# A decoder layer on one core: v by the seven-product scheme, with sums of products formed in their PSUM banks

## The chip, the core and the metric

One core of one Trainium2 chip runs the whole program. The metric is the device time of one execution in microseconds (us). TensorE (PE) multiplies, VectorE (DVE), ScalarE (ACT) and GpSimd (POOL) do the elementwise work, SyncE (SP) issues most of the DMAs.

## The reference, cut to what matters

One layer on 1024 tokens of 1024 channels, all in fp32:

```python
u = rms_norm(x, norm_g)                      # (1024, 1024)
proj = u @ w_in                              # ten blocks of 1024 columns
xc, bg, cg, zc, q, k, v, za, g_conv, g_attn = split(proj)
y_conv = (silu(zc) * bg * causal_conv(cg * xc, conv_w)) @ w_out_conv
o = mixture_of_dilations(q, k, v)            # 16 heads of 64
y_attn = (silu(za) * o) @ w_out_attn
merged = sigmoid(g_conv + b1) * y_conv + sigmoid(g_attn + b2) * y_attn
return rms_norm(x + merged @ w_o, final_g)
```

The change is in the input projection `u @ w_in`: in the part that gives v, and in the nine other blocks of columns (the sections).

## The kernel before, in words

**Exact fp32 from pairs.** TensorE works on float32r operands. Every fp32 operand a is therefore split (`split`, L78 to L80) into a high part, cast by ScalarE, and a low part, the difference, by VectorE or GpSimd. A product of two operands is three matmuls: low times high, high times low, high times high.

**The stage of v** (about the first 130 us). Each of eight token tiles of 128 rows of x is normalised: ScalarE sums the squares, VectorE takes the reciprocal root in three small steps with a Newton step (`rstd_of`, L101 to L111) and scales the tile in two halves (L173); TensorE turns each half with four transposes (L176), and `split` stores the result in one of four quadrants of u transposed: b11 (channels 0 to 511, tokens 0 to 511), b12 (the same channels, tokens 512 to 1023), b21 and b22 (channels 512 to 1023). v = u w_v is then computed in four blocks of 256 columns, in each eight token tiles, for each eight steps of the contraction with three matmuls of 256 columns (L212 to L214): 4 x 8 x 8 x 3 = 768. ScalarE casts the result from PSUM, VectorE takes the low part, and a DMA stores both (L215 to L219). The weights of a block are loaded and split by `load_v`; the low parts of all of them but the first half of block 0 are GpSimd's. Behind the first four tiles of the last block `sums` (L182 to L200) forms, for a slice of 128 tokens, t1 = b12 - b11, t2 = b22 - t1, t3 = t1 - b11 and so on from the pairs; nine operations of VectorE, four casts of ScalarE, four low parts of GpSimd for each slice. t1 to t4 are operands of the sections.

**The sections.** `sec` computes two blocks of 128 output columns for all tokens by Strassen's scheme in Winograd's form: seven products of half the contraction and half the tokens in place of eight (84 matmuls of 512 columns, L250 to L252, for a pair; 36 pairs). Three products go to SBUF through ScalarE (`keep`, L255 to L258), four are added by VectorE to a stored one (`added`, L260 to L264), and three more additions combine the sums in SBUF (L271 to L273). Every product has a PSUM bank of its own (`bank()` hands out eight in turn).

**What follows** is the attention, 16 heads, then the merge of the two branches and the output projection; the change does not touch their code.

**What sets the order.** The Tile framework orders the instructions with its own simulation of the program (`schedule_with_timeline_sim=True`) and then gives each engine one list, which that engine works through strictly in order. So the place of an instruction in the list of its engine decides what it can hold up. DMAs of SP and POOL are issued in the order of those lists as well.

## Time and profile before

| | |
|---|---|
| median of 3 runs | 1351.56 us (1350.42 to 1355.43) |
| the profiled execution, span | 1349.6 us |
| TensorE busy | 1303.3 us, 97 % of the span, 6660 matmuls and transposes |
| VectorE, ScalarE, GpSimd busy | 915.8, 631.4, 265.3 us |
| mean granted TensorE clock | 0.987 of full speed |
| stage of v, from the first load to the first section | 0 to about 130 us |
| sections | about 130 to 820 us |

The profile is one execution; its span runs from the first to the last instruction and is 2.0 us below the median of the runs. Busy time is time in which an engine executes, so TensorE's 97 % leave 46.3 us in which it did not. The granted clock says how much of full speed the throttle allowed: 1.0 is 2.4 GHz, 0.5 is 1.2 GHz. In the lists below "L212" is line 212 of the kernel, `out<-in` are the program's names for the operands, and "[4.79 <-DVE v L80]" says that the engine waited 4.79 us and that the VectorE instruction of line 80 that wrote v ended the wait.

### The profile page before, as it was taken

Reading aid. Unit: us, or ns where it says so; the run is one execution under the profiler, and the core shown is the slowest. Engines: PE = TensorE matmul, PEld = TensorE weight load, DVE = VectorE, ACT = ScalarE, POOL = GpSimd, SP = SyncE. Lnnn points to the kernel's source line nnn. Section 1 sums busy time; section 2 is a strip of 40 time slices with the busy share of each in tenths; the row PEclk is TensorE's granted clock in tenths of the full one; section 3 lists DMA queues with packets and bytes.
Section 4 is the critical chain, followed back from the end, with each engine's and each line's share of the span. In section 5 each row is a group of like instructions: output and inputs, shape, how many; then the busy total and the mean of one; then the engine's idle time right before and its main releaser. Section 6 shows DMA issues by size and latency. Waiting matters only on the chain.

```text
span 1349.6 us, 18655 instructions
## 1 busy us (share of the span) xinstructions
PE 1303.3 (97%) x6660; PEld 1102.2 (82%) x6660; DVE 915.8 (68%) x1722; ACT 631.4 (47%) x1259; POOL 265.3 (20%) x191
## 2 busy tenths in 40 slices
PE   7988999999999999999999998799999999999997
PEld 7988888888888888887888886688888888788886
DVE  6486777777878788887766566576766776564325
ACT  5333444443534444343444466666777767332211
POOL 1153000000100101011000001534345446164000
PEclk8989999999999999999999999899999999999999
DMA  7214454441322223246332317976466565555302
GB/s 273 102 63 141 141 187 154 162 148 52 104 68 78 94 70 103 63 124 196 108 109 96 125 70 197 319 196 173 142 166 173 140 160 200 210 187 187 141 32 93
DMA packets 85892, 187.19 MB, mean 139 GB/s; under 512 B 8552, under 2 KB 33388, under 8 KB 85672
## 3 DMA queue, kind: packets, MB, share of 16 engines
q1 hardware_dynamic: 83000, 177.08, 42.4%
q0 software_dynamic: 2800, 8.94, 2.0%
q8 instruction: 52, 0.85, 0.3%
q14 instruction: 40, 0.33, 0.1%
HBM read 127.67 MB, written 58.31 MB: 138 GB/s over the span
## 4 chain that ended last, share of the span: by engine, by line
PE 85%; DMA 7%; DVE 4%; ACT 2%; issue 1%; POOL 0%; SPq 0%; DVEq 0%; ACTq 0%; POOLq 0%
PE bank L252 16%; PE bank L251 16%; PE bank L250 16%; PE bank L97 4%; PE bank L99 4%; PE bank L98 4%; PE bank L480 3%; PE bank L491 2%; PE bank L492 2%; PE bank L651 2%; PE bank L649 2%; PE bank L650 2%; PE bank L362 2%; PE bank L363 2%; PE bank L214 2%; PE bank L212 2%
## 5 line engine op out<-in xcount | busy, mean ns | idle before, releaser
L252 PE MATMUL bank<-t_hi,a_lo 128*128 128x512 f32 x576 | 223.6, 390 | 2.1 <-DVE a_lo L80 2.1
L250 PE MATMUL bank<-t_hi,a_hi 128*128 128x512 f32 x576 | 224.1, 389 | 0.0
L251 PE MATMUL bank<-t_lo,a_hi 128*128 128x512 f32 x576 | 224.1, 389 | 0.0
L250 PE MATMUL bank<-b_hi,a_hi 128*128 128x512 f32 x432 | 168.1, 389 | 0.0
L251 PE MATMUL bank<-b_lo,a_hi 128*128 128x512 f32 x432 | 168.1, 389 | 0.0
L252 PE MATMUL bank<-b_hi,a_lo 128*128 128x512 f32 x432 | 167.9, 389 | 0.0
L79 ACT CAST a_hi<-s 128x512 fp32r<-128x512 f32 x144 | 89.4, 621 | 138.9 <-PE bank L251 128.7
L80 DVE TENSOR_TENSOR a_lo<-s,a_hi 128x512 fp32r<-128x512 f32 x144 | 101.1, 703 | 68.9 <-ACT a_hi L79 68.3
L79 ACT CAST a_hi<-raw 128x512 fp32r<-128x512 f32 x108 | 67.0, 621 | 161.5 <-PE bank L251 146.5
L252 PEld LDWEIGHTS bank<-t_hi,a_lo 128*128 128x128 f32 x576 | 108.1, 188 | 25.3 <-DVE a_lo L80 2.9
L251 PEld LDWEIGHTS bank<-t_lo,a_hi 128*128 128x128 f32 x576 | 108.1, 188 | 22.5
L250 PEld LDWEIGHTS bank<-t_hi,a_hi 128*128 128x128 f32 x576 | 108.1, 188 | 22.4
L372 ACT ACTIVATE pr<-pr,nm 128x640 f32<-128x640 f32 (+7 forms) x128 | 100.1, 783 | 26.2 <-DVE nm L367 25.8
L263 DVE TENSOR_TENSOR sec_o<-bank,x 128x512 f32<-128x512 f32 x108 | 74.5, 690 | 43.2 <-PE bank L252 40.5
L367 DVE CUSTOM_DVE_ANT_0 pr<-bank,bias 128x512 f32<-128x512 f32 (+3 forms) x128 | 72.2, 570 | 41.8 <-PE bank L363 40.0
L252 PEld LDWEIGHTS bank<-b_hi,a_lo 128*128 128x128 f32 x432 | 81.1, 188 | 16.9
L251 PEld LDWEIGHTS bank<-b_lo,a_hi 128*128 128x128 f32 x432 | 81.1, 188 | 16.8
L250 PEld LDWEIGHTS bank<-b_hi,a_hi 128*128 128x128 f32 x432 | 81.1, 188 | 16.8
L480 PE MATMUL bank<-ident,pr 128*128 128x128 f32 x576 | 89.3, 277 | 1.2 <-ACT pr L372 1.0
L212 PE MATMUL bank<-v_hi,b_hi 128*128 128x256 f32 x256 | 75.0, 296 | 11.8 <-DVE v L80 9.7
L80 DVE TENSOR_TENSOR a_lo<-raw,a_hi 128x512 fp32r<-128x512 f32 x108 | 75.3, 697 | 14.5 <-ACT a_hi L79 14.5
L80 DVE TENSOR_TENSOR pp<-bank,pp 128x512 fp32r<-128x512 f32 x96 | 65.3, 689 | 19.8 <-ACT pp L79 19.1
(212 smaller groups left out, 2913.3 us busy)
## 6 DMA issues: line engine op xcount, KB each, us to landing
raw<-in_w_blk SPq DMA_DIRECT2D x72, 512.0 KB, 3.8
v_dram<-v SPq DMA_DIRECT2D x32, 256.0 KB, 2.2
qk_dram<-qk_hi SPq DMA_DIRECT2D x32, 256.0 KB, 3.1
qk_dram<-qk_lo SPq DMA_DIRECT2D x32, 256.0 KB, 2.9
q<-qk_dram SPq DMA_DIRECT2D x32, 256.0 KB, 6.2
kh<-qk_dram SPq DMA_DIRECT2D x32, 256.0 KB, 8.5
kl<-qk_dram SPq DMA_DIRECT2D x32, 256.0 KB, 7.4
g_dram<-sg SPq DMA_DIRECT2D x32, 256.0 KB, 2.0
```

Of the source, the lines that this page charges most:

```text
L79: nc.scalar.copy(hi, src)
L80: (eng or nc.vector).tensor_sub(lo, src, f(hi))
L97: nc.tensor.matmul(pt, whi[:, k, :], mhi[:, t], start=(k == 0), stop=False)
L98: nc.tensor.matmul(pt, whi[:, k, :], mlo[:, t], start=False, stop=False)
L212: nc.tensor.matmul(pv, mhi[:, kk, tt], hi[:, kk, :], start=(k == 0), stop=False)
L250: nc.tensor.matmul(pt, hi[:, k], mhi[:, k], start=k == 0, stop=False)
L251: nc.tensor.matmul(pt, hi[:, k], mlo[:, k], start=False, stop=False)
L252: nc.tensor.matmul(pt, lo[:, k], mhi[:, k], start=False, stop=k == H - 1)
L263: nc.vector.tensor_add(o, pt, v)
L367: nc.vector.tensor_tensor_reduce(pr[:, c0:c0 + m], sc[:, :m], bias[hd][:, off:off + m], 1.0, 3.0e38 if nm is None else nm, OP.add, OP.min, ...
L372: nc.scalar.activation(pr[:, :nk], pr[:, :nk], AF.Exp, bias=nm, scale=-1.0, accum_out=den[p][:, a, b:b + 1])
L480: nc.tensor.transpose(pt[:, j, i * P:(i + 1) * P], rows[b][:, (kb + j) * P:(kb + j + 1) * P], ident)
```

## The change

It does four things.

1. **v by the seven-product scheme.** The products now have 512 columns: a product is half of the contraction (four steps) for four token tiles and 512 columns of v, 4 x 4 x 3 = 48 matmuls, and seven products make 336. The first two (b11 and b21 with the weights' first column half) are done tile by tile, in turn with the normalisation of tiles 0 to 3; then tiles 4 to 7 are normalised, within `sums`, and the other five products follow, each for all four tiles. Weights are loaded in pieces of two contraction steps by 512 columns, and VectorE forms their sums.
2. **Sums of products in their banks.** A product may go on adding to a bank that has been read already: `start` is set on the first product alone. In v and in every pair of columns of the sections the scheme then needs three banks (`chain`, `side`, `own`): chain holds x1, then x1 + x6 (t2's product is added), then t3's, then t4's. Four additions of VectorE go in each pair, and ScalarE copies one more value (u2).
3. **u's sums from fp32 copies.** For tiles 4 to 7 ScalarE copies the transposed tile out of PSUM (c12, c22), and `sums` forms t1, t2 and t3 from these. b12 has no pair any more. Six operations of VectorE for a slice remain, besides the normalisation.
4. **Memory.** Two pools are gone, x tiles have three buffers instead of four, and `dynamic_dma_scratch_size=4096` is set.

The diff, cut to its core (the sums' arithmetic and the helpers stand in full, unchanged lines mostly left out):

```diff
...
-        def load_v(c):
-            wv[c] = []
-            raw = [wr.tile([P, H, 256], F32, name="raw") for _ in range(2)]
...
+        def piece(c, d, kh):
+            raw = wr.tile([P, 2, 512], F32, tag="raw", name="raw")
+            k = 4 * d + 2 * kh
+            nc.sync.dma_start(raw, w_v[c, :, k:k + 2, :])
+            return raw
+        def operand(raw, eng=None):
+            hi = p0.tile([P, 2, 512], F32R, name="v_hi", bufs=4)
+            lo = p0.tile([P, 2, 512], F32R, name="v_lo", bufs=4)
+            split(hi, lo, raw, eng)
+            return hi, lo
...
+        raws = [piece(0, 0, 0), piece(0, 0, 1)]
         load_x(1)
+        raws += [piece(0, 1, 0), piece(0, 1, 1)]
+        load_x(2)
+        a1 = [operand(r, nc.gpsimd if i else nc.vector) for i, r in enumerate(raws)]
...
         def sums(j):
+            c12 = p0.tile([P, H, P], F32, name="c12", bufs=1)
+            c22 = p0.tile([P, H, P], F32, name="c22", bufs=1)
+            for n, pt in enumerate(normed(H + j)):
+                nc.scalar.copy(c22 if n else c12, pt)
+                if n:
+                    into("b22", j, pt)
+            t1, t2, t4 = (p0.tile([P, H, P], F32, name="ts", bufs=3) for _ in range(3))
+            b11, b21 = of("b11", j), of("b21", j)
+            nc.vector.tensor_sub(t1, c12, b11[0])
+            nc.vector.tensor_sub(t1, t1, b11[1])
+            into("t1", j, t1, nc.gpsimd)
+            nc.vector.tensor_sub(t2, c22, t1)
+            into("t2", j, t2, nc.gpsimd)
+            nc.vector.tensor_sub(c12, c22, c12)
+            into("t3", j, c12, nc.gpsimd)
+            nc.vector.tensor_sub(t4, b21[0], t2)
+            nc.vector.tensor_add(t4, t4, b21[1])
+            into("t4", j, t4, nc.gpsimd)
...
+                nc.tensor.matmul(pt, bhi[:, k, tt], hi[:, i, :], start=first and k == 0, stop=False, **more)
...
+        for j in range(H):
+            for n, pt in zip(("b11", "b21"), normed(j)):
+                into(n, j, pt)
+            for kh in range(2):
+                prod(chain[j], "b11", j, kh, a1[kh], first=True)
+            x1.append(p0.tile([P, 512], F32, name="keep1", bufs=4))
+            nc.scalar.copy(x1[j], chain[j])
+            pt = bank(4, 2)
+            for kh in range(2):
+                prod(pt, "b21", j, kh, a1[2 + kh], first=True)
+            added(0, j, pt, x1[j])
+        sum_ = []
+        for kh in range(2):
+            r1, r2 = piece(1, 0, kh), piece(1, 1, kh)
+            nc.vector.tensor_add(r1, r1, r2)
+            sum_.append(r1)
+        for j in range(H):
+            sums(j)
...
+        product("t1", side, [operand(r) for r in sum_], first=True)
...
+        product("t2", chain, [operand(r) for r in sum_])
...
+        product("b22", side, [operand(r) for r in sum_])
+        for j in range(H):
+            added(0, H + j, side[j], u2[j])
...
+        product("t3", chain, ops)
+        for j in range(H):
+            added(1, H + j, chain[j], x5[j])
+        product("t4", chain, [operand(piece(1, 1, kh)) for kh in range(2)])
+        for j in range(H):
+            emit(1, j, chain[j])
...
-        x1 = keep("x1", a11, "b11")
-        yield 0, T1, added(a12, "b21", x1)
-        x5 = keep("x5", sm["s1"], "t1")
-        x7 = keep("x7", sm["s3"], "t3")
-        u2 = added(sm["s2"], "t2", x1)
-        nc.vector.tensor_add(x7, x7, u2)
-        nc.vector.tensor_add(u2, u2, x5)
-        nc.vector.tensor_add(x5, x7, x5)
-        yield 1, T2, x5
-        yield 1, T1, added(a22, "t4", x7)
-        yield 0, T2, added(sm["s4"], "b22", u2)
+        chain = bank()
+        prod(chain, a11, "b11", first=True)
+        x1 = keep("x1", chain)
+        own = bank()
+        prod(own, a12, "b21", first=True)
+        yield 0, T1, added(own, x1)
+        side = bank()
+        prod(side, sm["s1"], "t1", first=True)
+        x5 = keep("x5", side)
+        prod(chain, sm["s2"], "t2")
+        u2 = keep("u2", chain)
+        prod(side, sm["s4"], "b22")
+        yield 0, T2, added(side, u2)
+        prod(chain, sm["s3"], "t3")
+        yield 1, T2, added(chain, x5)
+        prod(chain, a22, "t4")
+        yield 1, T1, chain
...
-        "w_v": blocks(w_in[:, 6 * D:7 * D], 256),
+        "w_v": blocks(w_in[:, 6 * D:7 * D], 512),
...
-    nc = _bacc.Bacc("TRN2", target_bir_lowering=False, num_devices=1)
+    nc = _bacc.Bacc("TRN2", target_bir_lowering=False, num_devices=1, dynamic_dma_scratch_size=4096)
...
```

Line numbers in the lists of the changed kernel are those of its own code: L103 to L110 are `rstd_of`, L171 scales a tile, L79 takes a low part, L226 is `added` of v (vc is the sum, keep_212 the stored x1), L245, L262, L269 and L276 form sums of weights, L194 to L202 stand in `sums`, L314 to L316 are a section's three matmuls.

**First place: VectorE between the token tiles.** Before, from its list at tile 2, with the low part of v (v_425, straight from PSUM) of column block 0 in between:

```order
L111 TENSOR_SCALAR rs<-rs_t,rs_y 128x1
L104 TENSOR_SCALAR rs_a<-ss 128x1
L80 TENSOR_TENSOR v_425<-bank,v_425 128x4x64
L173 SCALAR_TENSOR_TENSOR xt<-xt,rs,gb 128x512 x2
L80 TENSOR_TENSOR b_lo<-bank,b_hi 128x4x128
L108 RECIPROCAL rs_y<-rs_r 128x1
L80 TENSOR_TENSOR b_lo<-bank,b_hi 128x4x128 x2
L110 SCALAR_TENSOR_TENSOR rs_t<-rs_y,rs_a 128x1
L80 TENSOR_TENSOR b_lo<-bank,b_hi 128x4x128
L111 TENSOR_SCALAR rs<-rs_t,rs_y 128x1
```

With the change, the list between tiles 0 and 1 and on to the addition of tile 1:

```order
L226 TENSOR_TENSOR vc<-bank,keep_212 128x512
L245 TENSOR_TENSOR raw<-raw 128x1024
L103 TENSOR_SCALAR rs_a<-ss 128x1
L79 TENSOR_TENSOR v_229<-vc,v_229 128x8x64
L107 RECIPROCAL rs_y<-rs_r 128x1
L109 SCALAR_TENSOR_TENSOR rs_t<-rs_y,rs_a 128x1
L110 TENSOR_SCALAR rs<-rs_t,rs_y 128x1
L245 TENSOR_TENSOR raw<-raw 128x1024
L171 SCALAR_TENSOR_TENSOR xt<-xt,rs,gb 128x512 x2
L79 TENSOR_TENSOR b_lo<-bank,b_hi 128x4x128 x2
L226 TENSOR_TENSOR vc<-bank,keep_276 128x512
```

What reads the products of one tile (L226, then its low part L79) now stands ahead of the scaling (L171) of the next tile; before, the normalisation was a tile ahead.

**Second place: VectorE behind tile 3.** With the change, the list between the addition for tile 3 (its low part is v_421) and the first sum of u (ts<-c_435,b_hi); ahead of these rows stand, behind tile 3's b_lo, two weight steps L262, three low parts of weights and the addition itself:

```order
L103 TENSOR_SCALAR rs_a<-ss 128x1
L79 TENSOR_TENSOR v_421<-vc,v_421 128x8x64
L269 TENSOR_TENSOR raw<-raw 128x1024
L103 TENSOR_SCALAR rs_a<-ss 128x1 x2
L79 TENSOR_TENSOR v_lo<-raw,v_hi 128x1024
L107 RECIPROCAL rs_y<-rs_r 128x1 x3
L269 TENSOR_TENSOR raw<-raw 128x1024
L109 SCALAR_TENSOR_TENSOR rs_t<-rs_y,rs_a 128x1 x3
L110 TENSOR_SCALAR rs<-rs_t,rs_y 128x1 x3
L171 SCALAR_TENSOR_TENSOR xt<-xt,rs,gb 128x512 x6
L276 TENSOR_TENSOR raw<-raw 128x1024
L194 TENSOR_TENSOR ts<-c_435,b_hi 128x512
```

Four weight steps and the scaling of three tiles stand between the end of tile 3 and the first sum; before, the sums had all of u's tiles ready and stood among the last block's tiles.

**Third place: TensorE within a section.** Before, t2's product ended and t4's began in another bank (1554, 1582):

```order
L251 MATMUL bank_1554<-t2_lo_101,a_hi_1550 128x512
L252 MATMUL bank_1554<-t2_hi_100,a_lo_1551 128x512
L250 MATMUL bank_1582<-t4_hi_104,a_hi_1578 128x512
L251 MATMUL bank_1582<-t4_lo_105,a_hi_1578 128x512
L252 MATMUL bank_1582<-t4_hi_104,a_lo_1579 128x512
```

With the change t3's and t4's products are both in bank 2016. t3's last row stands 14 rows ahead of t4's first, which is the last but one here; between them are 12 matmuls of the next pair's b11 and two of its b21:

```order
L314 MATMUL bank_2179<-b11_hi_92,a_hi_2180 128x512
L315 MATMUL bank_2179<-b11_lo_93,a_hi_2180 128x512
L316 MATMUL bank_2179<-b11_hi_92,a_lo_2181 128x512
L314 MATMUL bank_2198<-b21_hi_94,a_hi_2199 128x512
L315 MATMUL bank_2198<-b21_lo_95,a_hi_2199 128x512
L314 MATMUL bank_2016<-t4_hi_104,a_hi_2145 128x512
L315 MATMUL bank_2016<-t4_lo_105,a_hi_2145 128x512
```

VectorE reads bank 2016 in between (the addition of x5), and TensorE's list has 14 matmuls of other banks to cover that.

## Rows read from the trace of the kernel before

**Rows 1.** The page, part 1: busy time, share of the span, instructions of each engine.

```profile
PE 1303.3 (97%) x6660; PEld 1102.2 (82%) x6660; DVE 915.8 (68%) x1722; ACT 631.4 (47%) x1259; POOL 265.3 (20%) x191
```

**Rows 2.** Windows: stretch, its length, busy PE, PEld, DVE, ACT, POOL; clock, DMA share, GB/s.

```profile
9.00:23.70 14.70, 10.84 (x59) 9.71 (x60) 12.41 (x26) 10.95 (x21) 4.73 (x2) 0.77 0.89 334
23.70:65.00 41.30, 41.26 (x347) 40.98 (x346) 21.48 (x51) 16.11 (x36) 6.03 (x3) 1.00 0.36 125
65.00:130.40 65.40, 55.66 (x430) 55.03 (x429) 47.13 (x53) 19.36 (x39) 28.67 (x18) 0.92 0.31 105
130.40:820.00 689.60, 687.46 (x3036) 568.68 (x3035) 520.94 (x784) 301.74 (x507) 30.74 (x27) 1.00 0.35 111
820.00:880.00 60.00, 47.20 (x274) 38.85 (x273) 35.56 (x124) 40.21 (x96) 25.37 (x12) 0.92 1.03 293
```

**Rows 3.** TensorE's waits, 0 to 131 us: total us, count, longest.

```profile
PE bank L212 <- DVE v L80: 9.7, 3, 4.8
```

**Rows 4.** Groups by line and form, whole span: busy us, mean ns, idle before.

```profile
L212 PE MATMUL bank<-v_hi,b_hi 128*128 128x256 f32 x256 | 75.0, 296 | 11.8 <-DVE v L80 9.7 <-ACT b_hi L79 2.0
L176 PE MATMUL bank<-ident,xt 128*128 128x128 f32 x64 | 9.6, 292 | 3.2 <-DVE xt L173 3.2
```

**Rows 5.** Timeline of PE, 83 to 90 us: start, duration, instruction, wait before it.

```profile
83.89 0.58 PE L212 MATMUL bank<-v_hi,b_hi 128*128 128x256 f32 x1 [4.79 <-DVE v L80]
...
88.54 0.36 PE L212 MATMUL bank<-v_hi,b_hi 128*128 128x256 f32 x1
88.74 0.28 PE L213 MATMUL bank<-v_lo,b_hi 128*128 128x256 f32 x1
88.86 0.28 PE L214 MATMUL bank<-v_hi,b_lo 128*128 128x256 f32 x1
```

**Rows 6.** Timeline of PE in a section, at 200 us.

```profile
199.88 0.39 PE L250 MATMUL bank<-t_hi,a_hi 128*128 128x512 f32 x1
200.11 0.39 PE L251 MATMUL bank<-t_lo,a_hi 128*128 128x512 f32 x1
```

**Rows 7.** Timeline of POOL, 0 to 46 us.

```profile
11.06 2.38 POOL L80 TENSOR_TENSOR v_lo<-raw,v_hi 128x1024 fp32r<-128x1024 f32 x1 [8.13 <-ACT v_hi L79]
```

**Rows 8.** Groups by line and form: an addition from PSUM on VectorE.

```profile
L263 DVE TENSOR_TENSOR sec_o<-bank,x 128x512 f32<-128x512 f32 x108 | 74.5, 690 | 43.2 <-PE bank L252 40.5
```

**Rows 9.** Groups by line and form: copies and casts of ScalarE.

```profile
L257 ACT COPY x<-bank 128x512 f32<-128x512 f32 x108 | 62.6, 580 | 0.0
L79 ACT CAST t_hi<-raw 128x512 fp32r<-128x512 f32 x16 | 9.9, 620 | 29.4 <-DVE raw L190 12.2 <-DVE raw L197 9.9 <-DVE raw L193 7.2
```

**Rows 10.** Timeline of VectorE, 0 to 46 us: normalisation of the first tile, a low part.

```profile
7.51 0.16 DVE L108 RECIPROCAL rs_y<-rs_r 128x1 f32<-128x1 f32 x1
...
8.20 1.42 DVE L173 SCALAR_TENSOR_TENSOR xt<-xt,rs,gb 128x512 f32<-128x512 f32 x2
9.73 1.23 DVE L80 TENSOR_TENSOR v_lo<-raw,v_hi 128x1024 fp32r<-128x1024 f32 x1
```

**Rows 11.** Timeline of VectorE, 91 to 108 us: the sections' sums.

```profile
91.40 1.77 DVE L188 TENSOR_TENSOR raw<-b_hi 128x512 f32<-128x512 f32 x1
...
102.49 1.71 DVE L188 TENSOR_TENSOR raw<-b_hi 128x512 f32<-128x512 f32 x1
...
105.91 2.71 DVE L190 TENSOR_TENSOR raw<-raw 128x512 f32<-128x512 f32 x1
```

**Rows 12.** Timeline of POOL, 98 to 108 us: low parts beside them.

```profile
99.13 1.35 POOL L80 TENSOR_TENSOR t_lo<-raw,t_hi 128x512 fp32r<-128x512 f32 x1 [1.28 <-ACT t_hi L79]
...
105.29 2.79 POOL L80 TENSOR_TENSOR v_lo<-raw,v_hi 128x1024 fp32r<-128x1024 f32 x1
```

**Rows 13.** DMA issues: queue, count, KB each, us to landing.

```profile
raw<-in_w_blk SPq DMA_DIRECT2D x72, 512.0 KB, 3.8
...
gc<-g_dram POOLq DMA_DIRECT2D x16, 256.0 KB, 3.3
```

**Rows 14.** TensorE's waits in the sections, 131 to 819 us: total us, count, longest.

```profile
PE bank L252 <- DVE a_lo L80: 2.1, 1, 2.1
```

More of the change, by code (lines that the diff above doesn't have):

```diff
@@ L202, in layer @@
[L202 to L221 removed]
+                yield pt
@@ new lines, in prod @@
+        def prod(pt, n, j, kh, op, first=False):
+            tt = slice(j * P, (j + 1) * P)
+            bhi, blo = ub[n]
+            hi, lo = op
+            for i in range(2):
+                k = 2 * kh + i
+                more = dict(skip_group_check=not first)
+                nc.tensor.matmul(pt, bhi[:, k, tt], hi[:, i, :], start=first and k == 0, stop=False, **more)
+                nc.tensor.matmul(pt, bhi[:, k, tt], lo[:, i, :], start=False, stop=False, **more)
+                nc.tensor.matmul(pt, blo[:, k, tt], hi[:, i, :], start=False, stop=k == H - 1, **more)
@@ new lines, in emit, with added @@
+        def emit(c, t, v):
+            v2 = p0.tile([P, 8, 2, HD], F32R, name="v2")
+            split(v2[:, :, 0, :], v2[:, :, 1, :], v.rearrange("p (h d) -> p h d", h=8))
+            nc.sync.dma_start(
+                v_dram[4 * c:4 * c + 4, :, t * 256:(t + 1) * 256].rearrange("n p e -> p n e"),
+                f(v2).rearrange("p (n a) s d -> p n (a s d)", n=4))
+        def added(c, t, pt, v):
+            vc = p0.tile([P, 512], F32, name="vc")
+            nc.vector.tensor_add(vc, pt, v)
+            emit(c, t, vc)
@@ new lines, in layer @@
+        chain = [ps.tile([P, 512], F32, tag=f"bank{j}", name="bank") for j in range(H)]
+        x1 = []
+        for j in range(H):
[9 more added lines that the diff above has]
+            added(0, j, pt, x1[j])
@@ new lines, in layer, with product @@
+        sum_ = []
[5 more added lines that the diff above has]
+            sums(j)
+        def product(n, pts, ops, first=False):
+            for kh in range(2):
+                for j in range(H):
+                    prod(pts[j], n, j, kh, ops[kh], first)
+        side = [ps.tile([P, 512], F32, tag=f"bank{4 + j}", name="bank") for j in range(H)]
+        product("t1", side, [operand(r) for r in sum_], first=True)
@@ new lines, in layer @@
+        x5 = []
+        for j in range(H):
+            x5.append(p0.tile([P, 512], F32, name="keep1", bufs=4))
+            nc.scalar.copy(x5[j], side[j])
+        for kh in range(2):
+            nc.vector.tensor_sub(sum_[kh], sum_[kh], piece(0, 0, kh))
+        product("t2", chain, [operand(r) for r in sum_])
+        u2 = []
+        for j in range(H):
+            u2.append(p0.tile([P, 512], F32, name="keep2", bufs=4))
+            nc.scalar.copy(u2[j], chain[j])
+        for kh in range(2):
+            nc.vector.tensor_sub(sum_[kh], piece(0, 1, kh), sum_[kh])
@@ new lines, in layer @@
+        product("b22", side, [operand(r) for r in sum_])
+        for j in range(H):
+            added(0, H + j, side[j], u2[j])
+        ops = []
+        for kh in range(2):
+            r1, r2 = piece(0, 0, kh), piece(1, 0, kh)
+            nc.vector.tensor_sub(r1, r1, r2)
+            ops.append(operand(r1))
+        product("t3", chain, ops)
+        for j in range(H):
+            added(1, H + j, chain[j], x5[j])
+        product("t4", chain, [operand(piece(1, 1, kh)) for kh in range(2)])
@@ L224, in layer @@
+        for j in range(H):
+            emit(1, j, chain[j])
     T1, T2 = slice(0, 512), slice(512, 1024)
@@ L247, in prod, with keep, added @@
             mhi, mlo = ub[b]
-            pt = bank()
             for k in range(H):
-                nc.tensor.matmul(pt, hi[:, k], mhi[:, k], start=k == 0, stop=False)
-                nc.tensor.matmul(pt, hi[:, k], mlo[:, k], start=False, stop=False)
-                nc.tensor.matmul(pt, lo[:, k], mhi[:, k], start=False, stop=k == H - 1)
-            return pt
-        def keep(name, a, b):
+                more = dict(skip_group_check=not first)
+                nc.tensor.matmul(pt, hi[:, k], mhi[:, k], start=first and k == 0, stop=False, **more)
+                nc.tensor.matmul(pt, hi[:, k], mlo[:, k], start=False, stop=False, **more)
+                nc.tensor.matmul(pt, lo[:, k], mhi[:, k], start=False, stop=k == H - 1, **more)
+        def keep(name, pt):
             v = pa.tile([P, 512], F32, name=name)
-            nc.scalar.copy(v, prod(a, b))
+            nc.scalar.copy(v, pt)
             return v
-        def added(a, b, v):
-            pt = prod(a, b)
+        def added(pt, v):
             o = pa.tile([P, 512], F32, name="sec_o", bufs=3)
```

81 lines of the change are left out of this document (15 added, 66 removed).

## The prediction, made before the changed kernel ran

> **What bounds the kernel now.** I read the page's busy shares first, then the stages, then the waits of the stage that the change rewrites. TensorE is busy 1303.3 of 1349.6 us [rows 1]: only what shortens or lengthens its work or its waits counts. By stages [rows 2], the sections (130.4 to 820) keep it busy 687.5 of 689.6 us, with VectorE at 520.9 and ScalarE at 301.7: TensorE is the bound there and the others have room. The stage of v (9.0 to 130.4) is different: TensorE is busy 107.8 of 121.4 us and twice below full clock (0.77 and 0.92). Its longest named wait is for VectorE, 9.7 us in three pieces [rows 3]: the sums for the sections hold VectorE up, and the copies out of PSUM stand behind them.
>
> **The products of v.** Removed: 768 matmuls of 256 columns (256 to a line, three lines [rows 4]). Added: seven products of four token tiles, four contraction steps and three matmuls, 336 of 512 columns. At full clock the 256-column ones start 0.12 us apart [rows 5], the 512-column ones 0.227 [rows 6]. So 92.2 us become 76.2: **16.0 us less**, if TensorE is kept fed. The 64 transposes stay.
>
> By the Trainium skill (TensorE: Matmul & The Clock Gate, "Back-to-back issue gap") a warm matmul costs its columns over 2.4 GHz plus 2.5 ns; that estimate gives 83.9 and 72.5 us, a gain of 11.4, and the forecast would be 4.6 us later. The rows are slower per matmul at both widths, so they decide.
>
> **How TensorE is fed now, in four pieces.** The order decides this, and all durations below are rows of before.
>
> *Tile 0.* The first product can start as now, at 11.6 us. But v's operands are four pieces, and GpSimd makes three of the low parts, where before it made one: from 11.06 on, 2.38 us each [rows 7], to 18.2. Then five of the second product's matmuls remain, 1.1 us at full clock, 2.1 at half: tile 0 ends at about 20.
>
> *Tiles 1 to 3.* The addition of tile j stands on VectorE ahead of the normalisation of tile j+1, and waits for tile j's last matmul; the transposes of j+1 wait for that normalisation. Between the tiles there thus stand: an addition from PSUM, 0.69 [rows 8]; ScalarE's rounding of it, 0.62 [rows 9]; the low part, 0.69; three small steps, 0.69 from the first's start to the scaling's (7.51 to 8.20), and half the scaled tile, 0.71 [rows 10]: 3.4 us, with handovers 3.6. Four transposes, then the other half and its four, make it 4.85 before products start again. The 24 products take 5.4. A tile takes 10.3 us, of which 4.0 are lost; before tile 1 also stand two weight additions of 1024 columns, 1.23 each (the row of a low part of that size [rows 10]). End of tile 3: 20 + 12.8 + 2 x 10.3 = 53.4.
>
> The clock adds to this. After a wait of 4.8 us the 22 matmuls from 83.89 to 88.54 started 0.21 us apart [rows 5], half rate: 2.0 us lost. I take three such losses, one for each gap between tiles: tile 3 ends at 59. The low end is none (53), the high end 61.
>
> The skill's section "HAM oscillation — how this bites in real kernels" on the same page says that a wait between short bursts can make every burst start at half clock. By that all three gaps pay, as I take it; the row shows it for one gap of 4.8 us, and two of the new gaps are some 4.
>
> *The hole behind tile 3.* The weight work for t1 and t2 and the normalisation of three tiles stand ahead of tile 4's sums on VectorE. From 0.7 us after tile 3's end: the addition 0.69, three low parts or weight steps of 1.23, one small, the low part of v 0.69, one more weight step 1.23, five small ones, another 1.23, six small ones: 11.2 us to the first scaled half, when tile 4's transposes come. Five more halves (3.5), a weight step (1.23), two subtractions and a low part from PSUM (2.1), ScalarE's cast (0.62) and handovers: t1's first product starts **19 us** after tile 3. TensorE has some 2 us of transposes to do in that time.
>
> *The sums.* A VectorE operation on two SBUF operands and a GpSimd one exclude each other: a subtraction that takes 0.69 alone took 2.71 and ended 0.5 us after the GpSimd operation beside it [rows 11, 12]. Both engines carry the sums, now 6 VectorE operations and 4 of GpSimd (1.3 us each [rows 12]) for a tile, where before there were 9 and 4. Before, one tile took 11.1 us (first subtractions at 91.40 and 102.49 [rows 11]); three operations fewer make 9.0. Tile 4's first subtraction stands 16.1 us behind tile 3, so tile 7's at 16.1 + 27 + 1.4 for its own scaling = 44.5. From there two subtractions, a cast and three GpSimd steps with VectorE's between are 7 us, and the last ten matmuls of t2 2.3: 54 us behind tile 3.
>
> *The rest.* Three products, 144 matmuls of 0.227, are 32.6 us; the first waits some 1.4 for a low part that VectorE makes behind the last sum. That is 88 behind tile 3. Weight loads (3.8 us to landing [rows 13]) are issued early enough. Handover: the first section's operand is cast behind the last tile of v (0.62 + 0.62), and VectorE has a low part, two sums and another low part to do (2.8); six products cover 1.4. Cost 2.0. The sections start 90 us behind tile 3, at **149** with tile 3 at 59, where before they started at 130.4: **18.6 us later**.
>
> **The sections.** 36 pairs of 84 matmuls, unchanged: 685.5 us of 0.227. Off VectorE go four operations of 0.69 in each pair, 99 us; one copy more lies on ScalarE (0.58 [rows 9], 21 us). Both lie under TensorE, which waited once, 2.1 us [rows 14]: gain 0 to 2.1, I take 0. The new waits are within a bank: t2 behind x1's copy, b22 behind x5's, t3 behind u2's, t4 behind VectorE's addition. The order has 12 or more matmuls (2.7 us) of another bank in each, against a copy and a cast, 1.2 us, or 0.8 for the addition. Without that cover t4 alone would cost 36 x 0.8 = 29 us. From 0 to 29, I take 0, by the nearest row, the one wait of 2.1 in all sections.
>
> **Memory and DMA.** The pools and GpSimd's smaller DMA scratch move every address. Between 820 and 880 TensorE idles 12.8 us behind loads (DMA share 1.03 [rows 2]); the same bytes come after, so 5 us either way, 0 taken. GpSimd's own loads in the merge land in 3.3 us [rows 13]; no row shows them waiting for room.
>
> **Sum.** 1349.6 + 18.6 = 1368.2 on the profiled execution's span. The median of the runs, 1351.6, lies 2.0 above it, so I add that: **1370 us**.
>
> **Rivals.**
> A, the other side: **TensorE stays fed.** Lost between tile 0 and the sections are, by the above, 14.4 in the gaps (4.0 three times and the two weight additions), 6 of clock, 17 in the hole, 12 under the sums, 3.4 behind them: 53 us. Would VectorE run ahead during the products, the stage could end, with none of them left, at 9.0 + 76.2 + 9.6 for the transposes [rows 4] + 5 for tile 0's waits = 100, which is 30 us earlier: 1321. It decides where fewer than some 30 of the 53 are left. For it: from 23.7 to 65 TensorE idled 0.04 us while VectorE normalised [rows 2]. Against it: there the normalisation stood ahead of what waits for products, and TensorE had other columns of v to turn to; here both queues alternate. Chance 0.20, between 1321 and 1344.
> B, **half of it**: gaps as reckoned, but the hole or the sums shorter by 10 to 25 us, since part of that work fits under tile 3's products and the clock does not fall. 1345 to 1358. Chance 0.11.
> C, **the sections wait within their banks**: on top of the forecast 28 us, about 1398, if another wait of VectorE's (a low part behind a store) stands ahead of the addition that t4 needs. Against it: the 3.2 us in between and VectorE's lower load. Chance 0.07.
> D, smaller: GpSimd's loads wait for scratch in the merge, or the loads at 820 come later; some 1385 to 1390. Chance 0.03.
>
> **The numbers.** The forecast has 0.59. Its own range: tile 3 at 53 and 86 behind it, 139, is 9 later than now; tile 3 at 61 and sums at the old pace, 9.0 + 2.1 three times, with 92 behind it, 159, is 29 later: 1360 to 1381. Measurements here can tell about 0.5%, 6.8 us. The range for 8 in 10 adds B, the upper 0.08 of A (9 of its 23 us) and most of D, and leaves out 0.12 of A, C and the end of D, 0.2: **1335 to 1388**. Faster 0.20 (A), same 0.11 (B), slower 0.69 (the forecast, C and D).
>
> **What would show it.** Right: TensorE idle some 4 us before the transposes of tiles 1 to 3, with VectorE's low part and scaling as releasers; a stretch of some 17 us with 16 transposes alone; t1 and t2 in pieces released by GpSimd; then about 33 us without a gap; first section near 149; sections 686 to 690 us long with TensorE full. Granted clock near 0.5 in pieces before 80 us. Wrong: if the sections start before 130 (A), if their length exceeds 695 us with waits for VectorE's additions (C), or if the stretch from the sections' end to the end of the span moves by over 6 us.

## The result, and the profile after

The change took 1376.6 us (median of 4 runs, 1373.71 to 1380.34) against 1353.3 for the kernel before on the same chip: the ratio is 1.017, with a 95% interval of 1.0145 to 1.0194. It is **23.3 us slower**, 6.6 us above the forecast (1.7 of that is the kernel before, which had been at 1351.6). The profiled execution is the slowest of the four, 1380.3 us with a span of 1378.5, so its differences against [rows 1] sum to 28.9 and not to 23.3.

The page, part 1, of the changed kernel:

```profile
PE 1304.9 (95%) x6228; PEld 1080.1 (78%) x6228; DVE 843.0 (61%) x1576; ACT 645.8 (47%) x1265; POOL 257.8 (19%) x187
```

TensorE has 432 instructions fewer than in [rows 1], which is 768 less 336, and VectorE works 72.8 us less. TensorE's busy time is still 1.6 us longer: what the matmuls that left would have saved was for the most part paid back by matmuls at half rate (the granted clock of the changed stage up to the first section is 0.85 on the mean). The stretches show where (stretch, its length, busy PE, PEld, DVE, ACT, POOL, granted clock, DMA share, GB/s):

```profile
20.00:60.00 40.00, 27.47 (x101) 20.65 (x99) 19.89 (x35) 12.55 (x22) 0.00 (x0) 0.83 0.38 124
60.00:85.00 25.00, 10.89 (x39) 8.23 (x40) 23.14 (x41) 12.23 (x26) 5.97 (x4) 0.59 0.46 146
85.00:125.00 40.00, 35.46 (x145) 26.93 (x144) 31.25 (x33) 21.08 (x33) 18.70 (x12) 0.96 0.27 88
...
160.00:840.00 680.00, 677.71 (x2986) 560.58 (x2985) 430.52 (x628) 298.80 (x500) 31.64 (x26) 1.00 0.34 111
```

Between 60 and 85 us VectorE is busy for 23.1 of 25.0 us and TensorE for 10.9, at a clock of 0.59. Before, the stage of v had no such stretch [rows 2]. From 160 to 840, in the sections, TensorE is full as before, and VectorE's share has fallen from 76% to 63%.

TensorE's timeline (start, duration, instruction, and in brackets the idle time ahead of it) has the stage in eight rows:

```profile
20.64 0.40 PE L215 MATMUL bank<-v_hi,b_lo 128*128 128x512 f32 x1
26.16 1.94 PE L174 MATMUL bank<-ident,xt 128*128 128x128 f32 x8 [5.13 <-issue]
39.38 1.94 PE L174 MATMUL bank<-ident,xt 128*128 128x128 f32 x8 [3.65 <-issue]
51.25 1.33 PE L174 MATMUL bank<-ident,xt 128*128 128x128 f32 x8 [3.64 <-issue]
70.45 2.88 PE L174 MATMUL bank<-ident,xt 128*128 128x128 f32 x12 [10.49 <-issue]
78.10 0.79 PE L213 MATMUL bank<-v_hi,t_hi 128*128 128x512 f32 x1 [0.93 <-ACT t_hi L78]
145.84 0.40 PE L215 MATMUL bank<-v_hi,t_lo 128*128 128x512 f32 x1
149.36 0.79 PE L314 MATMUL bank<-b_hi,a_hi 128*128 128x512 f32 x1 [3.13 <-ACT a_hi L78]
```

Tile 0 ends at 20.9; ahead of the transposes of tiles 1, 2 and 3 TensorE is idle for 5.13, 3.65 and 3.64 us; tile 3 ends at 59.8; t1's first product starts at 78.1; the last product of v ends at 146.1, and the first section starts at 149.36. "issue" stands where the profile names no releaser. VectorE's list names it (timeline of VectorE):

```profile
47.71 0.69 DVE L226 TENSOR_TENSOR vc<-bank,keep 128x512 f32<-128x512 f32 x1 [5.04 <-PE bank L215]
48.32 0.14 DVE L103 TENSOR_SCALAR rs_a<-ss 128x1 f32<-128x1 f32 x1
49.09 0.69 DVE L79 TENSOR_TENSOR v<-vc,v 128x512 fp32r<-128x512 f32 x1 [0.62 <-ACT v L78]
...
49.89 0.22 DVE L109 SCALAR_TENSOR_TENSOR rs_t<-rs_y,rs_a 128x1 f32<-128x1 f32 x1
...
50.39 1.42 DVE L171 SCALAR_TENSOR_TENSOR xt<-xt,rs,gb 128x512 f32<-128x512 f32 x2
```

The addition waited 5.04 us for tile 2's last matmul, and the scaling of tile 3, whose transposes start at 51.25, stands behind it and five more rows (L103, L79, L107, L109, L110).

By stages, in the profiled executions (start of the first section, length of the sections, from their last matmul to the end):

| | sections start | sections | behind them | span |
|---|---|---|---|---|
| before | 130.5 | 689.8 | 529.4 | 1349.6 |
| the change | 149.4 | 697.8 | 531.3 | 1378.5 |
| difference | +18.9 | +8.1 | +1.9 | +28.9 |

### The profile page after: what moved, and what is told of

It is laid out like the page before. It is cut to its first block, busy times and chain, and to the rows that moved or that the text cites. A ratio compares the mean times of both kernels' runs of the same rounds, so it can differ in the third digit from the quotient of the medians.

```text
span 1378.5 us, 17657 instructions
## 1 busy us (share of the span) xinstructions
PE 1304.9 (95%) x6228; PEld 1080.1 (78%) x6228; DVE 843.0 (61%) x1576; ACT 645.8 (47%) x1265; POOL 257.8 (19%) x187
## 4 chain that ended last, share of the span: by engine, by line
PE 85%; DMA 6%; issue 3%; ACT 3%; DVE 3%; POOL 0%; SPq 0%; DVEq 0%; ACTq 0%
PE bank L314 16%; PE bank L315 16%; PE bank L316 16%; PE bank L96 4%; PE bank L98 4%; PE bank L97 4%; PE bank L548 3%; PE bank L559 2%; PE bank L560 2%; PE bank L719 2%; PE bank L717 2%; PE bank L718 2%; PE bank L213 2%; DMA kl<-qk_dram 2%; PE bank L214 2%
## 5 line engine op out<-in xcount | busy, mean ns | idle before, releaser
L314 PE MATMUL bank<-t_hi,a_hi 128*128 128x512 f32 x576 | 225.2, 391 | 2.7 <-DVE sec_o L325 2.3
L316 PE MATMUL bank<-t_hi,a_lo 128*128 128x512 f32 x576 | 224.8, 390 | 0.0
L314 PE MATMUL bank<-b_hi,a_hi 128*128 128x512 f32 x432 | 169.5, 392 | 4.7 <-ACT a_hi L78 4.7
L316 PE MATMUL bank<-b_hi,a_lo 128*128 128x512 f32 x432 | 168.5, 390 | 0.0
L79 DVE TENSOR_TENSOR a_lo<-s,a_hi 128x512 fp32r<-128x512 f32 x144 | 102.1, 709 | 100.1 <-ACT a_hi L78 100.0
L314 PEld LDWEIGHTS bank<-t_hi,a_hi 128*128 128x128 f32 x576 | 108.5, 188 | 25.9 <-DVE sec_o L325 3.0
L316 PEld LDWEIGHTS bank<-t_hi,a_lo 128*128 128x128 f32 x576 | 108.4, 188 | 22.6
L314 PEld LDWEIGHTS bank<-b_hi,a_hi 128*128 128x128 f32 x432 | 81.6, 189 | 22.9 <-ACT a_hi L78 6.1
L79 DVE TENSOR_TENSOR a_lo<-raw,a_hi 128x512 fp32r<-128x512 f32 x108 | 74.3, 688 | 39.3 <-ACT a_hi L78 38.3
L316 PEld LDWEIGHTS bank<-b_hi,a_lo 128*128 128x128 f32 x432 | 81.5, 189 | 17.0
L79 DVE TENSOR_TENSOR pp<-bank,pp 128x512 fp32r<-128x512 f32 x96 | 64.9, 687 | 27.6 <-ACT pp L78 27.1
L430 PE MATMUL bank<-kh,q 128*128 128x256 f32 (+2 forms) x192 | 73.0, 382 | 5.8 <-DVE nm L435 2.1
L548 PEld LDWEIGHTS bank<-ident,pr 128*128 128x128 f32 x576 | 67.9, 141 | 12.3 <-ACT pr L440 6.5
```

Of the source, the lines that this page charges most:

```text
L79: (eng or nc.vector).tensor_sub(lo, src, f(hi))
L314: nc.tensor.matmul(pt, hi[:, k], mhi[:, k], start=first and k == 0, stop=False, **more)
L316: nc.tensor.matmul(pt, lo[:, k], mhi[:, k], start=False, stop=k == H - 1, **more)
L430: nc.tensor.matmul(sc[:, :n], qs, kh[hd][:, c0:c0 + n], start=True, stop=False)
L548: nc.tensor.transpose(pt[:, j, i * P:(i + 1) * P], rows[b][:, (kb + j) * P:(kb + j + 1) * P], ident)
```

## The experiments

**Which part of the change costs?** Two kernels took one half of it each. In the first, v and the sums are as before and only `sec` is new; in the second only `sec` is old.

```diff
 # v_old_sec_new: the kernel before, with the change's sec
-        x1 = keep("x1", a11, "b11")
...
+        chain = bank()
+        prod(chain, a11, "b11", first=True)
...
```

> The stage of v and its sums as before (v in four blocks of 256 columns), the sections with the sums of products in their banks. Theory (all of the loss is in the order of v's stage; the sections stay bound by TensorE): within 4 us of before, 1349 to 1357, first section near 130, sections 687 to 693 us long. Rival (the sections are some 8 us longer in the trace because t2, t3, t4 and b22 wait within their banks): 1359 to 1362, with waits for ScalarE's copies or VectorE's additions ahead of matmuls into a bank already used.

Measured: 1356.8 us, ratio to before 1.0015 (0.999 to 1.004). First section at 130.8, sections 692.3 long. TensorE's waits for additions came to 2.0 us in all sections, the longest 1.7. The rival is out at its size: the sums in their banks cost nothing that can be told from no change, and at most 0.4%.

```diff
 # v_new_sec_old: the change, with the sec of before
-        prod(chain, sm["s3"], "t3")
...
+        x7 = keep("x7", sm["s3"], "t3")
+        u2 = added(sm["s2"], "t2", x1)
...
```

> v's stage as in the change, the sections as before (a bank for each product, VectorE's additions). Theory: 1373 to 1380, first section at 148 to 151, the whole loss there. Rival (sections): 1366 to 1370. If VectorE's four extra operations for a pair matter, longer than the change.

Measured: 1378.9, ratio 1.0192 (1.0161 to 1.0223), first section at 151.8. The whole loss is there without the new sections, and 21 of it lie ahead of them in the profile. This kernel has the change's memory settings, too; they were not tried alone.

**Is it the order of VectorE's list?** The normalisation of a tile is written two tiles ahead of its products:

```diff
+        tile_of(0)
+        tile_of(1)
         for j in range(H):
-            for n, pt in zip(("b11", "b21"), normed(j)):
-                into(n, j, pt)
+            if j + 2 < H:
+                tile_of(j + 2)
```

> The change with the normalisation of a tile written two tiles ahead of its products, so that it stands ahead of the additions that wait for products. Theory (TensorE's three idle pieces before tiles 1 to 3, 12.4 us, and the half rate behind each, some 2 us, come from the addition standing ahead of the next tile's normalisation): tile 3 ends near 43 instead of 60 and the kernel takes 1358 to 1365. Rival (VectorE is the bound of the whole stage, so what is won ahead of tile 3 is lost behind it): 1373 to 1378, with the idle piece behind tile 3 longer by 12 to 17 us.

Measured: 1361.4, ratio 1.0056 (1.0037 to 1.0074), so **15 us of the 23 come back**. Tile 3 ends at 44.8 instead of 59.8, and the first section starts at 134.8 instead of 149.4. The trace:

```profile
20.17 0.63 PE L174 MATMUL bank<-ident,xt 128*128 128x128 f32 x4 [1.96 <-issue]
38.80 0.50 PE L213 MATMUL bank<-v_hi,b_hi 128*128 128x512 f32 x1 [0.24 <-ACT b_hi L78]
55.57 2.88 PE L174 MATMUL bank<-ident,xt 128*128 128x128 f32 x12 [10.63 <-issue]
```

Of the three idle pieces 1.96 us and 0.24 are left. The one behind tile 3 is as long as before the edit, 10.63 against 10.49, so nothing was given back there, against the rival.

**Can the idle piece behind tile 3 be taken away?** Three attempts. In the first, the eight sums of weights go from VectorE to GpSimd:

```diff
-            nc.vector.tensor_add(r1, r1, r2)
+            nc.gpsimd.tensor_add(r1, r1, r2)
...
```

> The change with the eight sums of v's weights on GpSimd instead of VectorE. Theory (the idle piece behind tile 3 is the length of VectorE's list there): seven operations of 1.23 us leave VectorE ahead of the first sum, 8 to 9 us less in all: 1366 to 1370. Rival (GpSimd's two-operand work holds VectorE up, as in the rows where a subtraction of 0.69 took 1.65, or a weight sum that waits for its load stands ahead of low parts of t1 to t4): 1374 or more.

Measured: 1378.7, ratio 1.0192 (1.016 to 1.0224), no gain: t1's first product starts at 77.8, against 78.1, and the first section at 154.6 instead of 149.4. The rival holds. VectorE's and GpSimd's timelines at the same times:

```profile
23.25 3.50 DVE L171 SCALAR_TENSOR_TENSOR xt<-xt,rs,gb 128x512 f32<-128x512 f32 x2
...
67.11 2.44 DVE L109 SCALAR_TENSOR_TENSOR rs_t<-rs_y,rs_a 128x1 f32<-128x1 f32 x2
```

```profile
23.80 2.40 POOL L245 TENSOR_TENSOR raw<-raw 128x1024 f32<-128x1024 f32 x1 [1.85 <-DMA raw<-in_w_v]
...
67.07 2.34 POOL L269 TENSOR_TENSOR raw<-raw 128x1024 f32<-128x1024 f32 x1 [1.76 <-DVE rs_a L103]
```

Two scaled halves, 1.42 alone [rows 10], took 3.50 beside a GpSimd sum; two steps on a single column, 0.22 each alone (49.89 above), took 2.44 and ended when GpSimd's sum did.

In the second, the weight pieces for t2, b22 and t3 are loaded only when a slice of t1 is there, on top of the normalisation ahead:

```diff
+            if after is not None:
+                nc.vector.tensor_copy(raw[:, 0, 0:1], after)
             nc.sync.dma_start(raw, w_v[c, :, k:k + 2, :])
...
```

> The normalisation two tiles ahead, and the weight pieces for t2, b22 and t3 loaded only when slices 0, 2 and 3 of t1 are there, so that their sums leave VectorE's list ahead of the first sum of u. Theory 1 (the idle piece behind tile 3 is a matter of order): 7 us less than with the normalisation ahead alone, 1352 to 1356. Theory 2 (VectorE's work is the length of everything from tile 3 to t2's end, so the weight sums only move behind and hold up the sums there): 1359 to 1363, the idle piece shorter by 5 to 8 us and the waits for t1 and t2 longer by as much.

Measured: 1374.2, ratio 1.0155 (1.0126 to 1.0185): slower than both theories said. t1's first product came at 56.4 instead of 62.9, so the idle piece did shrink by 6.5 us; the sections start at 137.4 instead of 134.8. So the order alone is not it (theory 1 falls). The weight sums of t2 and b22 now stand among u's sums, and one of t3's, behind them, waits for its late load:

```profile
105.24 1.23 DVE L283 TENSOR_TENSOR raw<-raw 128x1024 f32<-128x1024 f32 x1 [5.89 <-DMA raw<-in_w_v]
```

TensorE did not stop for that one. Its last matmul of v starts at 130.1 instead of 131.3, so 5.3 of the 6.5 us are lost again between t1 and there. The handover to the sections, 3.2 us of waiting with the normalisation ahead alone, then takes more than the rest:

```profile
PE bank L321 <- ACT a_hi L78: 6.9, 1, 6.9
```

The two profiled executions are 7.4 us apart, and 4.0 of that lie behind the sections; the medians are 13 apart, and the rest of that is not accounted for.

In the third, tile 4's normalisation and copies are written ahead of tile 3's products, too (the head of `sums` becomes a function of its own, `copies`):

```diff
...
+            if j == H - 1:
+                c4 = copies(0)
...
```

> As the one before, and tile 4's normalisation, its copies and its part of b22 written ahead of tile 3's products, where VectorE waits for TensorE. Theory 2 (only work put where VectorE idles shortens the stage): 4 to 6 us less than the one before, from the scaling and low part of a tile (2.1 us) and ScalarE's steps behind them. Theory 1: as the one before or up to 3 less.

Measured: 1368.3, ratio 1.0103 (1.008 to 1.0126): 6 us less than the one before, the size that theory 2 has, but not by its way. t1's first product starts at 50.3, 6.1 us earlier, the sections only 1.3 earlier, at 136.1, and they end at 834.2, against 833.8. What the profile gains lies behind the sections (531.7 us there instead of 535.5). That this edit shortens the stage on top of the late weights is not shown.

**The handover to the sections.** In the changed kernel ScalarE's list ends the stage like this:

```profile
146.46 0.58 ACT L78 CAST v<-bank 128x512 fp32r<-128x512 f32 x1 [2.40 <-DMA v_dram<-v]
148.21 0.58 ACT L78 CAST v<-bank 128x512 fp32r<-128x512 f32 x1 [1.17 <-DMA v_dram<-v]
148.69 0.62 ACT L78 CAST a_hi<-raw 128x512 fp32r<-128x512 f32 x1
151.19 0.62 ACT L78 CAST a_hi<-raw 128x512 fp32r<-128x512 f32 x1 [1.88 <-DMA v_dram<-v]
```

v has two buffers of 512 KB stores, and the casts of the last tiles wait for stores; the section's first cast stands behind them. The edit gives v the x tiles' buffers as well:

```diff
-            v2 = p0.tile([P, 8, 2, HD], F32R, name="v2")
+            xb = c == 1 and t not in (4, 5)
+            v2 = p0.tile([P, 8, 2, HD], F32R, name="v2", **(dict(tag="xt", bufs=3) if xb else {}))
```

> The change with five buffers instead of two for v's results in the last two products (three of them in the place of the x tiles, which are done by then). Theory (TensorE's 3.1 and 1.3 us ahead of the first section, and the half rate behind them, come from ScalarE's casts of the last v tiles waiting for earlier stores, with the section's first cast behind them): 3 to 5 us less than the change, 1371 to 1374, the first piece ahead of the sections under 1.5 us. Rival (VectorE's and ScalarE's own work there is as long as the stores): 1375 to 1378.

Measured: 1370.6, ratio 1.012 (1.0094 to 1.0146), 6 us less than the change. In the profiles the sections end 7.5 us earlier. TensorE's idle time ahead of the first section fell to 1.38 us, and the sections are 693.0 long instead of 697.8, as no half rate follows (the second matmul starts 0.33 us behind the first, against 0.60):

```profile
146.74 0.49 PE L315 MATMUL bank<-b_hi,a_hi 128*128 128x512 f32 x1 [1.38 <-ACT a_hi L78]
147.07 0.40 PE L316 MATMUL bank<-b_lo,a_hi 128*128 128x512 f32 x1
```

**Together.** First the edits of the third attempt and of the handover:

> The one before with five buffers for v's results as well: a candidate to beat the kernel before. If both hold, 1346 to 1354; if the handover gains nothing, as the one before.

Measured: 1360.6, ratio 1.0049 (1.003 to 1.0067). The handover gained 8 us here, and the sections end 7.4 earlier. The kernel before is not reached; the same kernel without the late weights takes 1355.7 (below), so they cost some 5 us.

Next the edits of the normalisation ahead and of the handover, without the late weights:

> The normalisation two tiles ahead and five buffers for v's results, nothing else. Theory (the two losses, ahead of tile 3 and at the handover to the sections, are separate and add): 1361 less 4 to 6, 1355 to 1357, no different from the kernel before. Rival (they overlap, as the first section waits for the same list of VectorE): 1359 to 1361.

Measured: 1363.0, ratio 1.0063 (1.0042 to 1.0083), no better than the normalisation ahead alone. In the trace both gains are there: sections at 132.4 instead of 134.8, 692.9 instead of 695.7 long. But 537.4 us lie behind the sections instead of 531.5, and TensorE's longest wait there is for a load, 5.6 us, where the other kernel waits 4.3 for the same one:

```profile
PE bank L96 <- DMA ghi<-y_dram: 5.6, 1, 5.6
```

The framework orders the whole program anew for each kernel: of TensorE's 2762 instructions behind the sections the first 243 are the same in both, and 1287 places hold another one. The medians, of 9 and 10 runs, point the same way as the profiles: less the end of the sections and 2.0, they leave 535.7 and 528.9 us, an estimate that takes the time up to there to be the same in every run. So the loss seems to go with this kernel; which part of the new order makes it is not shown.

With `c4 = copies(0)` as well:

> As the one before with tile 4's normalisation and copies ahead of tile 3's products, the weight sums left where the order puts them. Theory (VectorE's list up to t2's end decides; work put where VectorE waits for TensorE leaves that list): 2 to 4 us less, 1352 to 1355. Rival (the list has no such idle time left, or later tiles take it back): the same as the one before, 1354 to 1358.

Measured: 1355.7, ratio 1.0015 (0.9995 to 1.0035), 7 us less than without tile 4 ahead, more than the theory's 4. But in the profiles the sections end only 2.5 us earlier (822.8, against 825.3), which is the theory's size; 6.9 lie behind them, where the long stretch of the last kernel is gone again. It is level with the kernel before.

Without it, but with the low parts of the sums on VectorE:

```diff
-            into("t1", j, t1, nc.gpsimd)
+            into("t1", j, t1)
...
-            into("t4", j, t4, nc.gpsimd)
+            into("t4", j, t4)
```

> The normalisation two tiles ahead and five buffers, and the low parts of t1 to t4 on VectorE (0.69 each) instead of GpSimd. Theory (during the sums VectorE's and GpSimd's operations on SBUF exclude each other, so that VectorE loses some 2.6 us a tile in rows of 1.65 instead of 0.69): sixteen low parts add 11 us to VectorE and take 10 off, the same as without within 3 us, with no row of the sums over 0.8 us and a tile in 8 to 9 us. Rival (VectorE's number of operations alone is the bound): 8 to 11 us slower. Second rival (GpSimd's chain is the bound): 5 us faster or more.

Measured: 1352.1, ratio 0.9977 (0.996 to 0.9994): **11 us less**, of which the sums explain less than half. In the profiles the sections start 5.3 us earlier and end 4.3 earlier; 7.2 lie behind them, as with the kernel just above. The theory (the same within 3 us) is out by little up to there, the first rival (slower) falls. The second rival (5 us faster or more) has the size, but in the kernel it is compared with GpSimd waited 2.0 to 3.3 us for a cast in each tile but the first, so that its chain alone was the bound is not shown. From tile 4's first subtraction to tile 7's it takes 21.7 us (58.51 to 80.19) instead of 25.5 (59.90 to 85.35), and the last of these steps 6.7 instead of 8.2. VectorE beside GpSimd (first fence, the kernel with the normalisation ahead and five buffers) and alone (second fence):

```profile
80.93 1.57 DVE L201 TENSOR_TENSOR ts<-b_hi,ts 128x512 f32<-128x512 f32 x1
82.54 1.64 DVE L202 TENSOR_TENSOR ts<-ts,b_lo 128x512 f32<-128x512 f32 x1
...
85.35 1.75 DVE L194 TENSOR_TENSOR ts<-c,b_hi 128x512 f32<-128x512 f32 x1 [0.57 <-ACT c L189]
```

```profile
76.58 0.69 DVE L79 TENSOR_TENSOR t_lo<-ts,t_hi 128x512 fp32r<-128x512 f32 x1
77.19 0.69 DVE L79 TENSOR_TENSOR t_lo<-c,t_hi 128x512 fp32r<-128x512 f32 x1
77.79 0.69 DVE L201 TENSOR_TENSOR ts<-b_hi,ts 128x512 f32<-128x512 f32 x1
...
80.19 0.69 DVE L194 TENSOR_TENSOR ts<-c,b_hi 128x512 f32<-128x512 f32 x1
```

The theory's tile of 8 to 9 us went wrong in the price of an operation: rows of 0.69 start 0.60 apart when nothing else waits, so ten sums and low parts and one part of b22 are 6.6 us. It had taken 0.69 for each.

And all of these edits in one kernel:

> All that gained: the normalisation two tiles ahead and tile 4's ahead of tile 3's products, five buffers for v's results, the low parts of t1 to t4 on VectorE. Theory (both changes take work or waits out of one list of VectorE, and their 7 and 11 us add up to most of 18): 1343 to 1349, under the kernel before by over 0.3%, the first section at 120 to 124. Rival (the two overlap, since without GpSimd VectorE's list is full): 1350 to 1354.

Measured: 1351.1, ratio 0.9974 (0.9951 to 0.9997). It takes 25 us less than the change, and by the medians 0.3% less than the kernel before, with an interval that ends close to 1 (in these profiles it is 1.2 us longer). The time is the rival's, but the place is the theory's: the first section starts at 124.4. By stages, in the profiles:

| | sections start | sections | they end | behind them | span | median |
|---|---|---|---|---|---|---|
| before | 130.5 | 689.8 | 820.2 | 529.4 | 1349.6 | 1354.2 |
| normalisation ahead | 134.8 | 695.7 | 830.5 | 531.5 | 1362.0 | 1361.4 |
| and five buffers | 132.4 | 692.9 | 825.3 | 537.4 | 1362.7 | 1363.0 |
| these two, and tile 4 ahead | 130.8 | 692.0 | 822.8 | 530.5 | 1353.3 | 1355.7 |
| these two, and low parts on VectorE | 127.1 | 693.9 | 821.0 | 530.2 | 1351.3 | 1352.1 |
| all | 124.4 | 695.5 | 819.8 | 530.9 | 1350.8 | 1351.1 |

(The median of the kernel before is the one measured beside the last kernel.) Ahead of the sections the two gains, 1.6 and 5.3 us, add to 8.0 with both; to the end of the sections 2.5 and 4.3 come to 5.5. What the two kernels' gains of 7 and 11 us have in common, and what cannot be had twice, is the some 7 us behind the sections that the kernel with five buffers alone had lost. So that VectorE's full list makes the gains overlap, as the rival has it, is not what the traces show. It is full for a stretch: from 50 to 66 us it has no gap left (16.00 busy of 16.00), at a TensorE clock of 0.62:

```profile
50.00:66.00 16.00, 11.69 (x36) 8.13 (x36) 16.00 (x31) 6.76 (x15) 0.00 (x0) 0.62 0.42 135
```

## Why the prediction was right, and where its sizes were off

**The place and the mechanism hold.** The sections were forecast to start at 149 and started at 149.36. The pieces show that the terms hold, with errors of up to 1.4 us that in part cancel (the 1.4 us taken ahead of the last three products did not come at all); that the start agrees to 0.4 us is luck to that extent:

| piece | forecast | measured |
|---|---|---|
| tile 0 ends | 20 | 20.9 |
| idle ahead of tile 1 (with the two weight additions) | 6.1 | 5.13 |
| idle ahead of tiles 2 and 3, each | 3.6 | 3.65, 3.64 |
| tile 3 ends | 59 | 59.8 |
| from there to t1's first product | 19 | 18.3 |
| from tile 3's end to t2's end | 54 | 52.7 |
| the three products behind | 32.6 | 33.6 |
| handover | 2.0 | 3.3, and 3.6 inside the first section |

Moving the normalisation ahead took the idle pieces away and 15 us with them, so the order of VectorE's list, and not the products or the sections, is shown to be the cause of that part. The weight loads were taken to be early enough; one was not: in the idle piece behind tile 3 VectorE waits 1.42 us for a weight piece (the sum at 67.71).

**The products** start 0.233 us apart in v, not 0.227 as in a section [rows 6], which is 2 us over 336:

```profile
115.28 0.39 PE L214 MATMUL bank<-v_lo,b_hi 128*128 128x512 f32 x1
115.51 0.39 PE L215 MATMUL bank<-v_hi,b_lo 128*128 128x512 f32 x1
```

The warm gap of an isolated matmul in the Trainium skill (TensorE: Matmul & The Clock Gate, "Back-to-back issue gap"), 0.216 us for 512 columns by its formula, is not reached in either; the same section's sustained 0.131 still less.

**The clock.** Each of the three gaps between tiles was followed by half rate, as the forecast had chosen, but not by the same amount. Behind the first two the granted clock was 0.50 at the transposes already; behind the third it was 1.00 there and fell at the products (stretches at the transposes of tiles 2 and 3):

```profile
39.30:41.20 1.90, 1.82 (x9) 1.63 (x9) 0.72 (x2) 0.58 (x1) 0.00 (x0) 0.50 0.62 208
51.20:52.60 1.40, 1.28 (x9) 0.89 (x9) 0.68 (x2) 0.58 (x1) 0.00 (x0) 1.00 0.76 260
```

The rows behind the third gap:

```profile
52.55 0.67 PE L213 MATMUL bank<-v_hi,b_hi 128*128 128x512 f32 x1
53.02 0.63 PE L214 MATMUL bank<-v_lo,b_hi 128*128 128x512 f32 x1
53.45 0.63 PE L215 MATMUL bank<-v_hi,b_lo 128*128 128x512 f32 x1
```

These start 0.43 us apart, half rate, until 56.0. Against a start every 0.233 us the products of the three tiles lost 2.1, 0.7 and 1.6 us, and the transposes of the first two 0.5 each: some 5.3 us, where 6 were taken. Shorter idle pieces were followed by half rate, too: one of 2.57 us at 100.09 among the sums, and one of 1.99 in the sections (below). The Trainium skill (TensorE: Matmul & The Clock Gate, "HAM oscillation — how this bites in real kernels") says that such waits between short bursts make each burst start at half clock; this trace agrees for the gaps of 5.13 and 3.65 us, and for the one of 3.64 with the products only.

**The step that was mis-sized is the handover**: "Cost 2.0" measured 3.3 ahead of the first section, and 3.6 more in waits and half rate within its first ten matmuls, where the sum took nothing. The second of these waits:

```profile
151.87 0.79 PE L314 MATMUL bank<-b_hi,a_hi 128*128 128x512 f32 x1 [1.28 <-ACT a_hi L78]
```

The forecast reckoned VectorE's and ScalarE's operations and left out the stores of v, which hold the two buffers. The run with five buffers shows this: 6 us less, with 1.6 in place of the 3.3.

**The sections.** "I take 0" measured 8.1 us in the profile: 3.6 at the entry, 1.5 for half rate behind one wait, some 1.8 around seven transposes of the attention that stand between the last matmuls (two waits of 0.35 within a bank among it); the rest is small waits. Rival C is not borne out: with only the new sections the ratio is 1.0015, and a product's wait for an addition shows but once at any length in 36 pairs. The kernel before had one wait of 2.1 in its sections, for a low part [rows 14]. The one of the changed kernel:

```profile
631.64 0.50 PE L314 MATMUL bank<-t_hi,a_hi 128*128 128x512 f32 x1 [1.99 <-DVE sec_o L325]
```

One term of the reckoning was wrong without effect: ScalarE copies nothing more in a pair. u2 comes, but x7 goes, and the changed kernel has 72 copies to x and 36 to u where [rows 9] has 108:

```profile
L320 ACT COPY x<-bank 128x512 f32<-128x512 f32 x72 | 41.8, 580 | 0.0
L320 ACT COPY u<-bank 128x512 f32<-128x512 f32 x36 | 20.9, 580 | 2.3 <-PE bank L316 2.3
```

**The signs.** Of the signs named for being right, "t1 and t2 in pieces released by GpSimd" did not come: TensorE's waits among the sums are named for ScalarE's casts and VectorE's low part of b22, 2.57 us at 100.09, behind which, by the program, the bank of tile 7's transposes is free for t1. Nor are the sections 686 to 690 long; with 697.8 they pass the 695 set as a sign of C, but not with its waits.

**Rival A** needed fewer than some 30 of the 53 lost us to be left; in the change nearly all were there. But its point holds: VectorE can run ahead, when the program is written so. With its order mended, the buffers and GpSimd's low parts moved, the kernel comes to 1351.1. It did not come to 1321: its sections start at 124.4, where the rival has 100. VectorE being full from 50 to 66 is one part of that; the rest of the stage was not taken apart.

**Rivals B and D.** B falls: the idle piece behind tile 3 and the sums are as long as reckoned. For D the stretch behind the sections would have had to be 15 us longer; it is 1.9 longer.

**The sums.** 9.0 us a tile were taken; tile 4's first subtraction starts at 74.72 and tile 7's at 101.09, 8.8 a tile, in steps of 10.5, 7.7 and 8.2. (Before, t3 was t2 - b11, not t1 - b11; the count of nine operations stands.) GpSimd's part in it was seen as a constraint on VectorE only; that taking GpSimd out would shorten the phase was not foreseen.

## What to carry to other kernels

When an in-order engine must read a product and also prepare the next product's operand, look in its list for which comes first: with the reader first, TensorE idles for the whole preparation at each tile, and here it paid half rate behind it as well. Fewer matmuls do not help a stage whose length is another engine's list: add up that engine's rows from the last thing it waits for. When the whole program is ordered anew for each edit, check in the trace that the gain lies where the edit is. And at the end of a stage, count the buffers that stores still hold, as they sit in the same list as the next stage's first cast.

## What the runs showed of the hardware that was not expected

- GpSimd's low part of 1.3 to 1.7 us costs VectorE more than doing it itself in 0.60: with GpSimd 25.5 us from tile 4's first subtraction to tile 7's, without 21.7, though VectorE does four operations more for a tile.
- A step on a single column, 0.22 alone, took 1.24 us in the changed kernel while GpSimd was at work:

```profile
81.63 1.24 DVE L109 SCALAR_TENSOR_TENSOR rs_t<-rs_y,rs_a 128x1 f32<-128x1 f32 x1
```

- The time behind the sections, with the same code but an order made anew for each kernel, lay between 525.9 and 537.4 us in the profiles of the fourteen kernels. So a median that falls by 5 to 10 us does not show that an edit in the stage of v did it: read where the sections end, as well.
